# A 64 KiB input fetched by six transfers of 16, 8, 4, 2, 1 and 1 rows in place of one of 32 rows, beside an 8 MB load

## The chip, the cores and the metric

The kernel runs on one core of a Trainium2 chip. The metric is the device time of one execution in microseconds. The profile covers one execution; its span is about 2 us shorter than the time (782.8 against 784.6 us in the same execution). In the views DVE is VectorE, ACT is ScalarE, POOL is GpSimd and SP is SyncE; ACTq and SPq are what these two issue, and L57 is line 57 of that run's kernel.

## The reference

A mixture of four softmaxes: each of 32 x 128 positions has four rows of 4096 logits and four prior weights.

```python
logits: (32, 128, 4, 4096) float32      # 268 MB
prior:  (32, 128, 4)       float32      # 64 KiB
p   = softmax(prior,  axis=-1)          # over the 4 heads
s   = softmax(logits, axis=-1)          # over 4096
out = (p[..., None] * s).sum(axis=2)    # (32, 128, 4096) float32, 67 MB
```

## The kernel before

One batch is one 8 MB tile of 128 partitions x 4 heads x 4096. Each partition's part is one contiguous run of 64 KiB. Loads go through SyncE's DMA queue into two buffers, so the third load can start only when ScalarE has read the whole first tile. The prior goes through ScalarE's queue.

```python
    lpool = ctx.enter_context(tc.tile_pool(name="lpool", bufs=2))    # tiles of 8 MB
    epool = ctx.enter_context(tc.tile_pool(name="epool", bufs=2))    # results of the big Exps
    # ... cut
    load(0)                                             # SyncE's queue, 8 MB

    pr = cpool.tile([B, S, H], FP32, name="pr")
    nc.scalar.dma_start(out=pr, in_=prior)              # ScalarE's queue, 64 KiB
    load(1)                                             # SyncE's queue, 8 MB
    pmax = cpool.tile([B, S], FP32, name="pmax")
    nc.vector.reduce_max(pmax, pr, axis=AX.X)           # first reader of the prior
    pc = cpool.tile([B, S, H], FP32, name="pc")
    nc.vector.tensor_sub(pc, pr, pmax.unsqueeze(2).to_broadcast([B, S, H]))
    pe = cpool.tile([B, S, H], FP32, name="pe")
    nc.scalar.activation(pe, pc, AF.Exp)                # "the prior's Exp"
    # ... cut: sum, reciprocal and product pn, then 16 transposes of 32x32 into pp, all on VectorE

    for b in range(B):
        # ... cut: store(b - 1) from ScalarE's queue, the acc tile
        for h in range(H):
            # ... cut: et is a tile of epool, but for the last two batches
            nc.scalar.activation(et, lt[:, h], AF.Exp, accum_out=dsum)       # "big Exp"
            # ... cut
            nc.vector.reciprocal(rden, dsum)
            nc.vector.tensor_mul(coeff, rden, pp[:, h, b : b + 1])           # needs pp
            if h == 0:
                nc.vector.tensor_scalar_mul(out=acc, in0=et, scalar1=coeff)  # "the scaling"
            # ... cut: else acc = et * coeff + acc, "the accumulation"
        if b + 2 < B:
            load(b + 2)
        # ... cut: the last stores
```

The softmax here doesn't subtract the row's maximum and nothing guards it: scores larger than these inputs give would overflow.

## Time and profile before

| | before |
|---|---|
| time | 784.99 us, median of 3 runs (784.61 to 785.24) |
| DMA | 335.7 MB, 429 GB/s mean over the span |
| DVE busy / ACT busy | 70% / 60% |

These are lines of the page of before. The two rows of digits and numbers have 40 slices of the span. "DMA 73%" heads the chain of waits that ended last. The line of L60 is the reduce, the prior's first reader: after its busy time and mean stands its idle time and what ended it.

```profile
span 782.8 us, 977 instructions
...
DVE 544.9 (70%) x408; ACT 472.7 (60%) x258; POOL 0.2 (0%) x4
...
DMA  9999999999999999999999999999999999999997
GB/s 378 429 429 448 416 454 411 456 410 457 423 417 445 447 424 442 433 424 435 422 450 422 444 423 448 419 447 419 453 414 455 421 422 443 440 414 429 428 429 334
...
DMA 73%; DVE 18%; ACT 6%; issue 1%; DVEq 0%; ACTq 0%
...
L60 DVE TENSOR_REDUCE pmax<-pr 32x128 f32<-32x512 f32 x1 | 0.7, 673 | 11.5 <-DMA pr<-in_prior_dram 11.5
...
pr<-in_prior_dram ACTq DMA_DIRECT2D x1, 64.0 KB, 10.7
```

The DMA row is full in every slice but the last, while no compute engine is. A gap in this row cannot be made up later, because later slices have no room. The last line says that 64 KiB needed 10.7 us from issue to landing.

The next lines are of the timeline of before (start, duration, engine, what was done): the issues, the prior's reduce and transposes, then of the first batch the first big Exp, the scaling, the fourth big Exp and the store.

```profile
...
0.72 0.42 ACTq L57 DMA_DIRECT2D pr<-in_prior_dram  x1
0.73 39.20 SPq L45 DMA_DIRECT2D ltile<-in_logits_dram  x3
...
11.46 0.67 DVE L60 TENSOR_REDUCE pmax<-pr 32x128 f32<-32x512 f32 x1 [11.46 <-DMA pr<-in_prior_dram]
...
16.28 1.97 DVE L78 STREAM_TRANSPOSE pp<-pn 32x32 f32<-32x32 f32 x16
23.56 3.62 ACT L100 ACTIVATE etile<-ltile 128x4096 f32<-128x4096 f32 x1 [10.05 <-DMA ltile<-in_logits_dram]
...
27.70 2.35 DVE L106 TENSOR_SCALAR acc<-etile,coeff 128x4096 f32<-128x4096 f32 x1
...
35.87 3.62 ACT L100 ACTIVATE etile<-ltile 128x4096 f32<-128x4096 f32 x1 [1.40 <-DVE rden L103]
...
45.38 0.37 ACTq L51 DMA_DIRECT2D out_dram<-acc  x1
...
```

The first two loads keep the DMA engines full until about 42 us. The third load may go when the fourth big Exp has ended, at 39.5 us.

Below the views lie the trace's packet records (queue, start, duration, bytes; they do not name the engine). The prior's packets of before come in three rounds of 16, one per engine:

```
before, ScalarE's queue, by rounds
16 packets of 2048 B   start  4.75 to  5.50 us
16 packets of 2048 B   start  7.36 to  8.23 us
16 packets of    4 B   start 10.21 to 11.01 us    (the completions)
```

A completion is the 4-byte packet that follows an engine's rows; the prior's first reader starts 0.4 us after the last of them.

Between two rounds each engine moved one 64 KiB load packet (about 2.5 us; 2.42 us later, undisturbed). So a prior packet waits a "turn" of one load packet, whether it carries 2048 or 4 bytes.

### The profile page before, as it was taken

Reading aid. Unit: us, or ns where it says so; the run is one execution under the profiler, and the core shown is the slowest. Engines: PE = TensorE matmul, PEld = TensorE weight load, DVE = VectorE, ACT = ScalarE, POOL = GpSimd, SP = SyncE. Lnnn points to the kernel's source line nnn. Section 1 sums busy time; section 2 is a strip of 40 time slices with the busy share of each in tenths; the row PEclk is TensorE's granted clock in tenths of the full one; section 3 lists DMA queues with packets and bytes.
Section 4 is the critical chain, followed back from the end, with each engine's and each line's share of the span. In section 5 each row is a group of like instructions: output and inputs, shape, how many; then the busy total and the mean of one; then the engine's idle time right before and its main releaser. Section 6 shows DMA issues by size and latency. Waiting matters only on the chain.

```text
span 782.8 us, 977 instructions
## 1 busy us (share of the span) xinstructions
DVE 544.9 (70%) x408; ACT 472.7 (60%) x258; POOL 0.2 (0%) x4
## 2 busy tenths in 40 slices
DVE  3576687666786667866678666687666876669994
ACT  0766556755567555575555765556755567558971
POOL 0000000000000000000000000000000000000000
DMA  9999999999999999999999999999999999999997
GB/s 378 429 429 448 416 454 411 456 410 457 423 417 445 447 424 442 433 424 435 422 450 422 444 423 448 419 447 419 453 414 455 421 422 443 440 414 429 428 429 334
DMA packets 10712, 335.68 MB, mean 429 GB/s; under 512 B 1200, under 2 KB 1200, under 8 KB 1232
## 3 DMA queue, kind: packets, MB, share of 16 engines
q1 hardware_dynamic: 6624, 276.83, 82.0%
q10 hardware_dynamic: 4080, 58.79, 17.5%
q14 instruction: 8, 0.07, 0.0%
HBM read 268.50 MB, written 67.11 MB: 429 GB/s over the span
## 4 chain that ended last, share of the span: by engine, by line
DMA 73%; DVE 18%; ACT 6%; issue 1%; DVEq 0%; ACTq 0%
DMA ltile<-in_logits_dram 39%; DMA out_dram<-acc 34%; DVE acc L108 10%; ACT etile L100 6%; DVE ltile L108 3%; DVE acc L106 3%; DVE ltile L106 1%; DVE coeff L104 1%; DVE ltile L114 0%; DVE rden L103 0%; DVEq L152 0%; ACTq L100 0%; ACTq L51 0%; DVEq L106 0%
## 5 line engine op out<-in xcount | busy, mean ns | idle before, releaser
L100 ACT ACTIVATE etile<-ltile 128x4096 f32<-128x4096 f32 x120 | 433.4, 3612 | 276.3 <-DMA ltile<-in_logits_dram 203.9
L108 DVE SCALAR_TENSOR_TENSOR acc<-etile,coeff,acc 128x4096 f32<-128x4096 f32 x90 | 403.6, 4484 | 3.2
L103 DVE RECIPROCAL rden<-dsum 128x1 f32<-128x1 f32 x128 | 20.2, 158 | 156.3 <-ACT etile L100 156.3
L106 DVE TENSOR_SCALAR acc<-etile,coeff 128x4096 f32<-128x4096 f32 x30 | 70.6, 2353 | 50.1 <-DMA out_dram<-acc 50.0
L100 ACT ACTIVATE ltile<-ltile 128x4096 f32<-128x4096 f32 x8 | 28.9, 3610 | 4.8 <-DMA ltile<-in_logits_dram 2.2
L104 DVE TENSOR_TENSOR coeff<-rden,pp 128x1 f32<-128x1 f32 x128 | 20.4, 159 | 4.4
L108 DVE SCALAR_TENSOR_TENSOR ltile<-ltile,coeff 128x4096 f32<-128x4096 f32 x5 | 22.4, 4485 | 0.2
L100 ACT ACTIVATION_READ_ACCUMULATOR etile<-ltile 128x1 f32 x120 | 22.4, 186 | 0.0
L60 DVE TENSOR_REDUCE pmax<-pr 32x128 f32<-32x512 f32 x1 | 0.7, 673 | 11.5 <-DMA pr<-in_prior_dram 11.5
L64 ACT ACTIVATE pe<-pc 32x512 f32<-32x512 f32 x1 | 0.6, 628 | 10.4 <-DVE pc L62 10.4
L114 DVE SCALAR_TENSOR_TENSOR ltile<-ltile,coeff 128x1024 f32<-128x1024 f32 x4 | 4.9, 1281 | 0.0
L106 DVE TENSOR_SCALAR ltile<-ltile,coeff 128x4096 f32<-128x4096 f32 x2 | 4.7, 2353 | 0.1
L64 ACT ACT_TABLE_LOAD x1 | 1.3, 1283 | 1.2 <-PEq L141 1.2
L78 DVE STREAM_TRANSPOSE pp<-pn 32x32 f32<-32x32 f32 x16 | 1.9, 170 | 0.1
L100 ACT ACTIVATION_READ_ACCUMULATOR ltile<-ltile 128x1 f32 x8 | 1.5, 186 | 0.0
L66 DVE TENSOR_REDUCE psum<-pe 32x128 f32<-32x512 f32 x1 | 0.7, 674 | 0.7 <-ACT pe L64 0.7
L71 DVE TENSOR_TENSOR pn<-pe,prec 32x512 f32<-32x512 f32 x1 | 1.0, 1021 | 0.0
L68 DVE RECIPROCAL prec<-psum 32x128 f32<-32x128 f32 x1 | 0.9, 942 | 0.0
L62 DVE TENSOR_TENSOR pc<-pr,pmax 32x512 f32<-32x512 f32 x1 | 0.7, 678 | 0.0
L141 POOL MEMSET const-bfloat16-1.0<- 128x1 bf16 x1 | 0.1, 101 | 0.0
L141 POOL MEMSET const-uint8-127<- 128x1 uint8 x1 | 0.1, 101 | 0.0
L141 POOL MEMSET const-float32-0.0<- 128x1 f32 x1 | 0.1, 98 | 0.2 <-issue 0.2
(1 smaller groups left out, 0.1 us busy)
## 6 DMA issues: line engine op xcount, KB each, us to landing
out_dram<-acc ACTq DMA_DIRECT2D x28, 2048.0 KB, 30.0
ltile<-in_logits_dram SPq DMA_DIRECT2D x12, 2048.0 KB, 22.9
out_dram<-acc SPq DMA_DIRECT2D x2, 2048.0 KB, 34.1
out_dram<-ltile SPq DMA_DIRECT2D x1, 2048.0 KB, 22.8
out_dram<-ltile SPq DMA_DIRECT2D x2, 1024.0 KB, 10.2
ltile<-in_logits_dram SPq DMA_DIRECT2D x29, 31.3
pr<-in_prior_dram ACTq DMA_DIRECT2D x1, 64.0 KB, 10.7
```

The source lines that it names most:

```text
L60: nc.vector.reduce_max(pmax, pr, axis=AX.X)
L62: nc.vector.tensor_sub(pc, pr, pmax.unsqueeze(2).to_broadcast([B, S, H]))
L64: nc.scalar.activation(pe, pc, AF.Exp)
L68: nc.vector.reciprocal(prec, psum)
L71: nc.vector.tensor_mul(pn.rearrange("b h s -> b s h"), pe, prec.unsqueeze(2).to_broadcast([B, S, H]))
L78: nc.vector.transpose(pp[32 * t : 32 * (t + 1), h, :], pn[:, h, 32 * t : 32 * (t + 1)])
L100: nc.scalar.activation(et, lt[:, h], AF.Exp, accum_out=dsum)
L103: nc.vector.reciprocal(rden, dsum)
L104: nc.vector.tensor_mul(coeff, rden, pp[:, h, b : b + 1])
L106: nc.vector.tensor_scalar_mul(out=acc, in0=et, scalar1=coeff)
L108: nc.vector.scalar_tensor_tensor(out=acc, in0=et, scalar=coeff, in1=acc, op0=ALU.mult, op1=ALU.add)
L114: nc.vector.scalar_tensor_tensor(out=acc[:, cs], in0=et[:, cs], scalar=coeff, in1=acc[:, cs], op0=ALU.mult, op1=ALU.add,)
```

## The change

The intent: smaller first pieces, more transfers in flight, the same 64 KiB. Nothing else changes, and the order of all other instructions on all engines stays.

```diff
     pr = cpool.tile([B, S, H], FP32, name="pr")
-    nc.scalar.dma_start(out=pr, in_=prior)
+    for lo, hi in ((16, 32), (8, 16), (4, 8), (2, 4), (1, 2), (0, 1)):
+        nc.scalar.dma_start(out=pr[lo:hi], in_=prior[lo:hi])
     load(1)
```

## The prediction

> **What bounds the kernel now.** Data transfer. The page's DMA row is at nine tenths or more in all slices but the last, 429 GB/s mean for 335.7 MB; DVE is busy 70%, ACT 60%. The chain of waits is 73% DMA. In the trace's packet records a load packet is one 64 KiB row; an undisturbed one takes 2.42 us, so 16 engines give 433 GB/s, and 335.7 MB need 775 of the 782.8 us. A stretch with empty engines is paid in full. Before the third load, by the timeline, the first two loads keep the engines full until about 42 us, and ACT releases the third at about 39.5 us: a margin of 2.5 us.
>
> **What the change does.** No bytes go away. One DMA issue on ACT's queue (0.42 us) becomes six (about 2.5 us, while ACT has nothing to do: free). The order of the other instructions is unchanged; DMA semaphores are handed out five places later, but each is again met long after its earlier transfer landed: zero.
>
> The cost is the prior's landing, which competes with the first 8 MB load. In the packet records of before each engine carries two 2 KiB prior rows and one 4-byte completion, each behind one 64 KiB load packet, starting at about 4.9, 7.6 and 10.3 us; the reduce waits 11.46 us. This agrees with the Trainium skill, "DMA: Bandwidth & Descriptors", Queues, rings and completion order: engines alternate between queues packet by packet. The same page (Why a DMA increments its semaphore by 16) says that a transfer uses the largest engine count up to 16 that divides its slowest dimension, on the lowest-numbered engines. Then all six pieces put a row and a completion on the first engine: 12 packets instead of 3, each behind a load packet. No run has shown this yet.
>
> Estimate: from 4.9 us, 11 more turns at 2.4 to 2.85 us (one fewer where the load's own completion takes the turn): last completion at about 31.3 us, reduce at 31.7 us instead of 11.46.
>
> **On the critical path.** The prior's Exp stands before the first big Exp on ACT. Its chain (0.67+0.68+0.63 us) ends at about 33.8 us, so the first big Exp starts there, not at 23.56. The transposed prior is ready at about 38.5 us (18.25 before). Repeating the first batch's timeline (Exp 3.6, scale 2.35, accumulate 4.48, two Exp buffers), the fourth Exp ends at about 49.9 us instead of 39.5. The third load's packets start at about 51 us instead of 41.8: engines nearly empty for some 8.5 us from 42.5 us. The rest repeats shifted by about 9 us; nothing gives it back, as the engines are full to the end.
>
> **Prediction: 794.2 us**, 80% range 785.5 to 799.0. Faster by over 2%: 0.01. Within 2%: 0.92. Slower by over 2%: 0.07.
>
> **What would show it.** Right: the prior's reduce waits about 31.5 us; small prior packets spaced by a load packet until about 31 us; first big Exp at about 34 us; DMA share near zero from 43 to 51 us; busy times and the later 24 us per batch unchanged. Wrong step: the prior lands near 11 to 16 us (pieces not stacked, or several small packets per turn), and the time stays at 785. Wrong size: prior late, but the gap shorter, or later slices denser.
>
> **What would make it wrong.** Pieces might start on different engines; a turn may carry several small packets; a late start might find slack that I do not see. One-row pieces may be cut across all engines, which leaves the first engine's count.

## More of the kernel before

All runs quoted here are with a granted clock of 1.000.

The window view of before has, per window, the busy time of DVE, ACT and POOL, the clock, then the DMA share and GB/s:

```profile
...
core 0: us, DVE busy (x) ACT busy (x) POOL busy (x), PEclk, DMA share, GB/s
40.00:42.00 2.00, 1.93 (x4) 0.00 (x0) 0.00 (x0) 1.00 0.84 360
42.00:44.00 2.00, 2.00 (x1) 0.00 (x0) 0.00 (x0) 1.00 0.46 197
44.00:46.00 2.00, 1.35 (x1) 0.14 (x1) 0.00 (x0) 1.00 1.21 524
46.00:48.00 2.00, 0.00 (x0) 2.00 (x1) 0.00 (x0) 1.00 1.25 524
48.00:50.00 2.00, 0.33 (x3) 2.00 (x3) 0.00 (x0) 1.00 1.27 541
...
```

A packet is counted by its start, and a load packet of 64 KiB takes longer than a window. So single windows swing around 1. What matters is that none is near zero: the third load follows the second without a pause.

## The result, and the profile after

| | before | after |
|---|---|---|
| time, median of 4 | 784.89 us (784.61 to 785.24) | 793.52 us (793.24 to 795.87) |
| prior's reduce starts | 11.46 us | 30.59 us |
| transposed prior ready | 18.25 us | 37.40 us |
| first packet of the third load | 41.71 us | 49.75 us |

The ratio is 1.0116, 95% interval 1.0096 to 1.0136. A ratio here is the mean time of one kernel's runs over that of the other's of the same rounds, so it is not quite the ratio of the medians (1.0110). The change costs 8.6 us, 1.1%, which is within 2%.

The same lines of the page after. (The chain of waits is not shown: in this profile it can be followed back only through the last 6% of the span.)

```profile
span 791.9 us, 987 instructions
...
DVE 546.3 (69%) x408; ACT 470.9 (59%) x258; POOL 0.2 (0%) x4
...
DMA  9959999999999999999999999999999999999997
GB/s 377 467 218 424 409 444 456 405 459 414 445 420 444 436 434 420 428 460 408 454 411 449 435 425 456 418 434 417 456 410 454 414 444 449 415 421 434 427 430 331
...
L61 DVE TENSOR_REDUCE pmax<-pr 32x128 f32<-32x512 f32 x1 | 0.7, 675 | 30.6 <-DMA pr<-in_prior_dram 30.6
...
```

The reduce now waits 30.6 us, and the third slice of the DMA row falls to five tenths, 218 GB/s. All other slices of that row are as before; busy times of DVE and ACT differ by less than 2 us. From 60 to 720 us both kernels move 433 GB/s by the window view. So nearly all of the loss is one gap at the start.

The timeline after:

```profile
...
0.72 2.25 ACTq L58 DMA_DIRECT2D pr<-in_prior_dram  x6
0.73 48.39 SPq L45 DMA_DIRECT2D ltile<-in_logits_dram  x3
...
30.59 0.68 DVE L61 TENSOR_REDUCE pmax<-pr 32x128 f32<-32x512 f32 x1 [30.59 <-DMA pr<-in_prior_dram]
...
32.55 3.60 ACT L101 ACTIVATE etile<-ltile 128x4096 f32<-128x4096 f32 x1
...
35.44 1.96 DVE L79 STREAM_TRANSPOSE pp<-pn 32x32 f32<-32x32 f32 x16
...
37.83 2.35 DVE L107 TENSOR_SCALAR acc<-etile,coeff 128x4096 f32<-128x4096 f32 x1
...
45.06 3.62 ACT L101 ACTIVATE etile<-ltile 128x4096 f32<-128x4096 f32 x1 [1.07 <-DVE rden L104]
...
54.57 0.38 ACTq L51 DMA_DIRECT2D out_dram<-acc  x1
...
```

All of the first batch's compute is later, and the third load waits for it. The windows after:

```profile
...
core 0: us, DVE busy (x) ACT busy (x) POOL busy (x), PEclk, DMA share, GB/s
40.00:42.00 2.00, 1.93 (x4) 1.72 (x1) 0.00 (x0) 1.00 0.00 0
42.00:44.00 2.00, 2.00 (x1) 1.99 (x2) 0.00 (x0) 1.00 0.00 0
44.00:46.00 2.00, 1.93 (x4) 0.94 (x1) 0.00 (x0) 1.00 0.00 0
46.00:48.00 2.00, 2.00 (x1) 2.00 (x1) 0.00 (x0) 1.00 0.00 0
48.00:50.00 2.00, 1.97 (x3) 0.77 (x2) 0.00 (x0) 1.00 0.98 328
...
```

Four windows stand at zero, the first of them only because its packets had started before 40 us. By the packet records the second load's last packet ends at 42.05 us and the third load's first starts at 49.75 us: 7.7 us with empty engines, at a stage where before had none. Here is why the prior is late, from the records:

```
after, ScalarE's queue, by rounds
16 x 2048 B at  4.8-5.1     16 x 4 B at  7.5-7.9     (16 rows)
 8 x 2048 B at  9.9-10.3     8 x 4 B at 12.5-12.9    (8 rows)
 4 x 2048 B at 15.0-15.3     4 x 4 B at 17.6-17.8    (4 rows)
 2 x 2048 B at 20.0-20.1     2 x 4 B at 22.5-22.6    (2 rows)
 1 x 2048 B at 22.52         1 x 4 B at 25.02        (1 row)
 1 x 2048 B at 27.45         1 x 4 B at 29.94        (1 row)
```

Each transfer puts one row on each of as many engines as it has rows. The spacing stays that of a load packet, 2.4 to 2.7 us, all the way to the last completion: on the engine with most packets, 12 prior packets in ten such steps of 2.5 us on average and one step without a wait. This is what one finds if one engine takes part in all six transfers and alternates: one prior packet, one load packet. That one step, at 22.5 us, also fits: there the first load's own completion (4 bytes) took the load's turn.

### The profile page after: what moved, and what is told of

Read it like the earlier page. It is cut to its first block, busy times and chain, and to the rows that moved or that the text cites. A ratio compares the mean times of both kernels' runs of the same rounds, so it can differ in the third digit from the quotient of the medians.

```text
span 791.9 us, 987 instructions
## 1 busy us (share of the span) xinstructions
DVE 546.3 (69%) x408; ACT 470.9 (59%) x258; POOL 0.2 (0%) x4
## 3 DMA queue, kind: packets, MB, share of 16 engines
q10 hardware_dynamic: 4096, 58.79, 17.3%
## 5 line engine op out<-in xcount | busy, mean ns | idle before, releaser
L61 DVE TENSOR_REDUCE pmax<-pr 32x128 f32<-32x512 f32 x1 | 0.7, 675 | 30.6 <-DMA pr<-in_prior_dram 30.6
```

## The experiments

Theory ("turns"): a prior packet waits one load packet of its engine; the engine with the most prior packets decides when the prior has landed; from there a fixed chain of compute leads to the third load; past a break-even this opens a gap in the DMA, paid in full. Rivals: (A) each extra transfer costs by itself; (B) the six transfers shift the semaphores which later transfers use by five places, and this costs (a semaphore is what the program makes an engine wait on until a transfer has landed); (C) the gap comes from ScalarE's order, where the prior's Exp stands before the big ones; (D), which no run was made for: the six transfers do not share an engine but follow one another, each starting when the one before has wholly landed.

All outputs are right. All runs are in three rounds with the kernel before on the same chip. Four kernels of one submission (two34, fine6, fine1, spfirst6) were run by no chip the first time and were sent again, unchanged, as the runs ending in "b".

### Two transfers of 16 rows (two16)

```diff
-    for lo, hi in ((16, 32), (8, 16), (4, 8), (2, 4), (1, 2), (0, 1)):
+    for lo, hi in ((16, 32), (0, 16)):
```

> Two transfers of 16 rows. Turn theory (each packet of the prior waits one 64 KiB load packet on its engine; the engine with the most packets decides): 4 packets on every engine (row, completion, row, completion), starting at about 4.9, 7.5, 10.0 and 12.6 us, so the prior's reduce starts at about 13.2 us; break-even is a start at 22.5 us, so the time stays that of before, 785 us. Rival (each extra transfer costs by itself, 8.6 us over 5 extra ones = 1.7 us each): 786.6 us. Rival (the shifted semaphore places cost): some loss, of unknown size.

Measured: 785.15 us against 784.71; ratio 1.0011 (0.9994 to 1.0028): no cost. The reduce starts at 14.07 us, 0.9 us later than expected, as some turns took 2.9 us. One more turn is free, because the prior has slack.

### Four transfers, 8 packets on the busiest engine (four8)

```diff
-    for lo, hi in ((16, 32), (8, 16), (4, 8), (2, 4), (1, 2), (0, 1)):
+    for lo, hi in ((16, 32), (8, 16), (4, 8), (0, 4)):
```

> Four transfers of 16, 8, 4 and 4 rows. Turn theory: 8 packets on the first four engines, the last starting at about 22.5 us, the reduce at about 23.1 us, just past the break-even of 22.5 us: 785 to 786 us. Rival (cost per transfer): three extra transfers, 790.1 us, the same as the next run of four transfers.

Measured: 786.75 us against 784.71; ratio 1.0026 (1.0011 to 1.0041). The reduce starts at 23.68 us, the third load's packets at 42.85 us. This is 0.75 us above the range that was expected, and far below the 790.1 of rival A.

### Five transfers, 10 packets (five10)

```diff
-    for lo, hi in ((16, 32), (8, 16), (4, 8), (2, 4), (1, 2), (0, 1)):
+    for lo, hi in ((16, 32), (8, 16), (4, 8), (2, 4), (0, 2)):
```

> Five transfers of 16, 8, 4, 2 and 2 rows: 10 packets on the first two engines. Turn theory: last packet at about 25.0 us, reduce at about 25.6 us, 3.1 us past break-even, so the third load starts at about 44.8 us and the time is about 788.3 us (787.5 to 789). Rival (cost per transfer): 791.8 us.

Measured: 788.82 us against 784.71; ratio 1.0057 (1.0042 to 1.0072). The timeline of this run has the reduce where it was expected:

```profile
...
25.50 0.67 DVE L61 TENSOR_REDUCE pmax<-pr 32x128 f32<-32x512 f32 x1 [25.50 <-DMA pr<-in_prior_dram]
...
```

The third load's packets start at 44.66 us, as expected (44.8). Rival A's 791.8 us is off by 3 us. Dropping the last split of two rows into 1 and 1 thus saves 4.5 us of the 8.6, each against before in its own rounds.

The records of this run also speak against rival D. The fourth transfer's two completions start at 22.16 and 22.40 us, the fifth's two rows at 22.18 and 22.41 us. So the fifth transfer's first row starts before the fourth has wholly landed, and each row comes right behind one completion, as on a shared engine.

### Four transfers, 12 packets in count (four12): a miss

```diff
-    for lo, hi in ((16, 32), (8, 16), (4, 8), (2, 4), (1, 2), (0, 1)):
+    for lo, hi in ((7, 32), (3, 7), (1, 3), (0, 1)):
```

> Four transfers of 25, 4, 2 and 1 rows. 25 rows can be split over 5 engines only, so the first engine has 5+1, 1+1, 1+1 and 1+1 = 12 packets, as many as the changed kernel has with six transfers. Turn theory: last packet at about 30 to 30.5 us, reduce at 30.6 to 31.2 us, 793.5 to 794.5 us, as the changed kernel. Rival (cost per transfer): 790.1 us, the same as the run of 16, 8, 4 and 4 rows.

Measured: 785.05 us against 784.71; ratio 1.0008 (0.9993 to 1.0023). The theory's number failed by 9 us, and rival A's by 5. The packet records of the profiled run (its time was 786.72 us, the other three 784.65 to 785.33) show that 25 rows did go to five engines, five rows each, as expected, but not all of them waited:

```
four12, ScalarE's queue
20 x 2048 B at 1.69-3.28     5 x 2048 B at 5.5-5.8     then turns, last completion at 22.97
```

Twenty rows went at once, and then five together one load packet later. So four rows on each of five engines were on their way before those engines had started their first 64 KiB load packet. Four turns were saved, the reduce started at 23.64 us, and this run cost 2.0 us, as four8 with its 8 packets did. The three other runs cost nothing that shows; they left no trace, so what was different in them is not known. The count of packets was right, but "each behind a load packet" was not: packets that are there first wait for nothing.

### The same four transfers, held back (four12late), and their control (four8late)

Both kernels write the prior's tile once on VectorE and ScalarE first. Its transfers must wait for that, and are issued at 2.7 us and not at 0.7.

```diff
     pr = cpool.tile([B, S, H], FP32, name="pr")
+    nc.vector.memset(pr, 0.0)
+    nc.scalar.activation(pr, pr, AF.Exp)
-    for lo, hi in ((16, 32), (8, 16), (4, 8), (2, 4), (1, 2), (0, 1)):
+    for lo, hi in ((7, 32), (3, 7), (1, 3), (0, 1)):         # four12late
+    for lo, hi in ((16, 32), (8, 16), (4, 8), (0, 4)):       # four8late
```

> The run of 25, 4, 2 and 1 rows missed: in its records four of the five rows of the 25-row piece reached their engines before those had their first load packet, and passed without waiting, so only 8 of 12 packets took turns. Here the same four transfers are held until ScalarE has written the prior's tile once (a fill and an Exp, some 2 us), so that the load comes first. Turn theory: all 12 packets wait, the first starts at about 4.8 us or one turn later, the reduce at 30.5 to 33.5 us, the third load's packets 19.2 us after it, and 793.5 to 796.5 us. Rival (a count of packets or of engines does not matter, 25 rows are simply cheaper): 785 us.

> Control of the run before it: the same delay by ScalarE, and also four transfers, but of 16, 8, 4 and 4 rows, so 8 packets on the busiest engines. Turn theory: reduce at 23.5 to 26 us, 786.5 to 789 us, some 7 us less than the run before it. If the delay itself or the number of transfers made the time: the same time as that run.

Measured: four12late 797.34 us against 784.76, ratio 1.0177 (1.0132 to 1.0222; one of its runs took 802.85 us), which leaves open whether it is over 2%. four8late 786.99 us, ratio 1.0038 (1.0001 to 1.0076; one of its runs took 791.25 us). The reduce in the timelines of four12late and then of four8late:

```profile
...
33.28 0.68 DVE L63 TENSOR_REDUCE pmax<-pr 32x128 f32<-32x512 f32 x1 [31.90 <-DMA pr<-in_prior_dram]
...
23.85 0.67 DVE L63 TENSOR_REDUCE pmax<-pr 32x128 f32<-32x512 f32 x1 [22.48 <-DMA pr<-in_prior_dram]
...
```

Now all five rows of the 25-row piece wait: their rounds start at 7.2, 9.7, 12.2, 14.8 and 17.5 us, and the last completion at 32.63 us. The third load's packets start at 52.45 us. The reduce came within the range expected; the time is 0.8 us above it. With the same number of transfers and the same delay, 8 packets cost 2.2 us and 12 packets 12.6 us, a larger step than the 7 us expected. Number and delay of the transfers are excluded as the cause; how many turns are taken is what counts.

### 31 rows and 1 row (two34b)

```diff
-    for lo, hi in ((16, 32), (8, 16), (4, 8), (2, 4), (1, 2), (0, 1)):
+    for lo, hi in ((1, 32), (0, 1)):
```

> (Second try of the run of 31 and 1 rows, which no chip ran; since then the transfer of 25 rows has been measured to cost nothing, so the divisor reading is in doubt.) Two transfers of 31 and 1 rows. If the engine count is the largest divisor up to 16 of 31, which is 1, the first engine holds 34 packets: reduce at 43 to 46 us and 805 to 811 us. If odd row counts are split otherwise (near evenly over the engines, as few packets on each), the reduce starts at 13 to 16 us and the time is 785 us. Rival (cost per transfer): 786.6 us.

The doubt named there came from the times of four12 alone; its records settle it, as the 25 rows end in five completions. Measured: 808.14 us against 785.02; ratio 1.029 (1.0266 to 1.0314). Only two transfers, and the largest loss of all. The timeline:

```profile
...
44.52 0.67 DVE L61 TENSOR_REDUCE pmax<-pr 32x128 f32<-32x512 f32 x1 [44.52 <-DMA pr<-in_prior_dram]
...
```

The records show one prior packet at a time: 7 rows by 2.6 us, before the engine's first load packet, then one per turn from 5.38 us, and the last 9 rows within 0.7 us from 43.28 us, once the loads had nothing more to send. So all 31 rows sat on one engine, and turns, not bytes, took the time. The third load's packets start at 63.68 us.

### Six transfers beside small load packets (fine6b, control fine1b)

```diff
-    load(0)
+    lt = lpool.tile([P, H, V], FP32, name="ltile")
+    for c in range(0, V, V // 2):
+        nc.sync.dma_start(out=lt[:, :, c : c + V // 2], in_=logits[0, :, :, c : c + V // 2])
+    ltiles[0] = lt
     # fine6b: the six prior transfers as in the change; fine1b: one of 32 rows
```

> The six transfers of the changed kernel, but the first batch's load comes as two transfers of half the columns of each head, so its packets are 8 KiB and not 64 KiB (turn of about 0.3 us). Turn theory: the 12 packets of the first engine pass within some 4 to 6 us, the reduce starts at about 8 to 11 us and the time is that of before, 785 us. If the six transfers cost by their number, by their small size or by the semaphore places: still about 793.5 us.

> Control of the run before it: the same two column halves for the first load, and the prior in one transfer. Turn theory: reduce at 6 to 8 us, and 785 us, within 0.5 us of the run with six transfers. If the finer first load gains or loses time by itself, it shows here against the kernel before.

Measured: fine6b 785.87 us, ratio to before 1.0006 (0.9983 to 1.0028); fine1b 784.95 us, ratio 0.9992 (0.9970 to 1.0013). The timeline of fine6b:

```profile
...
9.11 0.67 DVE L64 TENSOR_REDUCE pmax<-pr 32x128 f32<-32x512 f32 x1 [9.11 <-DMA pr<-in_prior_dram]
...
```

With 8 KiB load packets the same six transfers have landed at 9.1 us and not at 30.6, and the loss is gone. In fine1b, the reduce starts at 2.55 us and not at the 6 to 8 us expected, because all its prior packets (1.76 to 2.14 us) start before the load's first (2.18 us); the time is that of before: an earlier prior gains nothing. In fine6b too the first transfer's rows and most of its completions start before the load's first packet (2.16 us), so the edit changed a second thing besides the packet size; but ten packets of the busiest engine still had to pass beside the load. They did not pass at one load packet each throughout: between the second transfer's last completion (4.32 us) and the third's first row (5.70 us) 69 load packets started, about four on each engine. Why is not known. The 0.9 us between fine6b and fine1b is above the 0.5 us that was expected; the intervals of both hold 1, and its cause is open. Rival A falls here, as it did in two34b: this kernel has all six transfers and even one more load transfer, without the loss.

### Six transfers ahead of the first load in its own queue (spfirst6b)

```diff
-    load(0)
     pr = cpool.tile([B, S, H], FP32, name="pr")
     for lo, hi in ((16, 32), (8, 16), (4, 8), (2, 4), (1, 2), (0, 1)):
-        nc.scalar.dma_start(out=pr[lo:hi], in_=prior[lo:hi])
+        nc.sync.dma_start(out=pr[lo:hi], in_=prior[lo:hi])
+    load(0)
```

> The six transfers issued from SyncE's queue ahead of the first load, so they stand before it in the same queue and nothing is to be waited for. Turn theory: reduce at about 5 to 6 us. The first load is issued 2.25 us later than before (six issues), so its packets and everything behind them start about 2.3 us later: 787 us (786.5 to 788). Rivals (number of transfers, semaphore places): 793.5 us or more.

Measured: 786.37 us against 785.02; ratio 1.0009 (0.9983 to 1.0035), a little under the range expected. The reduce is earlier than expected too:

```profile
...
3.98 0.68 DVE L60 TENSOR_REDUCE pmax<-pr 32x128 f32<-32x512 f32 x1 [3.98 <-DMA pr<-in_prior_dram]
...
```

The first load's packets start 2.0 us later than before (3.74 against 1.74 us); the median is 1.35 us above before's. Standing first in the queue cures nearly all of it. The semaphores of later transfers are shifted here too, and by the trace the transfers from the second load on use the same ones as in the changed kernel, so rival B falls with this run.

### Two big Exps ahead of the prior's Exp (expfirst6)

```diff
+    early = {}                                    # ahead of the prior's chain
+    for h in range(2):
+        # ... cut: tiles et and dsum, as in the loop
+        nc.scalar.activation(et, ltiles[0][:, h], AF.Exp, accum_out=dsum)
+        early[h] = et, dsum
+    # ... cut: tile zero
+    nc.vector.tensor_scalar_mul(out=zero, in0=early[1][1][:B], scalar1=0.0)
     pmax = cpool.tile([B, S], FP32, name="pmax")
     # ... cut
-    nc.scalar.activation(pe, pc, AF.Exp)
+    nc.scalar.activation(pe, pc, AF.Exp, bias=zero)
     # ... cut: for b == 0 and h < 2 the loop takes et and dsum from early
```

> The changed kernel with the first two big Exps ahead of the prior's Exp in ScalarE's order (a zero bias made from the second sum holds that order). It asks which part of the late prior delays the third load. If ScalarE's order is what binds, the first batch gains up to about 8 us and the time goes back towards 785 us. If VectorE's chain from the reduce to the transposed prior binds (the first scaling needs it, and the third big Exp needs the buffer that the scaling frees), the first Exp starts at 23.6 us, but the first scaling at about 38 us as in the changed kernel, the third load's packets at about 49.8 us, and the time stays at 793.5 to 794.5 us.

Measured: 794.85 us against 784.78; ratio 1.0127 (1.0111 to 1.0144), 0.35 us above the range expected if VectorE's chain binds. The timeline, with the two early Exps, the reduce, the first scaling and the fourth big Exp:

```profile
...
23.15 3.62 ACT L64 ACTIVATE etile<-ltile 128x4096 f32<-128x4096 f32 x1 [18.84 <-DMA ltile<-in_logits_dram]
...
26.76 3.60 ACT L64 ACTIVATE etile<-ltile 128x4096 f32<-128x4096 f32 x1
...
30.49 0.67 DVE L69 TENSOR_REDUCE pmax<-pr 32x128 f32<-32x512 f32 x1 [30.49 <-DMA pr<-in_prior_dram]
...
37.71 2.35 DVE L118 TENSOR_SCALAR acc<-etile,coeff 128x4096 f32<-128x4096 f32 x1
...
44.67 3.62 ACT L112 ACTIVATE etile<-ltile 128x4096 f32<-128x4096 f32 x1 [0.81 <-DVE rden L115]
...
```

The first big Exp starts 9.4 us earlier than in the changed kernel (23.15 against 32.55 us), yet the scaling starts at 37.71 against 37.83 us, and the third load's packets at 49.38 against 49.75 us. Rival C falls: ScalarE's idle time was the visible symptom, but the scaling waits for the transposed prior, and the third Exp for the buffer that the scaling frees.

### All runs on one line

| run | packets that took turns on the busiest engine | reduce starts | third load's first packet | difference | median, less before's |
|---|---|---|---|---|---|
| four8 | 8 | 23.68 us | 42.85 us | 19.17 | +2.0 us |
| four12, its profiled run | 8 | 23.64 us | 42.81 us | 19.17 | +2.0 us (the run; the median +0.3) |
| four8late | 8, first one turn later, last without a wait | 23.85 us | 43.02 us | 19.17 | +2.2 us |
| five10 | 10 | 25.50 us | 44.66 us | 19.16 | +4.1 us |
| changed kernel | 12 | 30.59 us | 49.75 us | 19.16 | +8.6 us |
| four12late | 12, first one turn later | 33.28 us | 52.45 us | 19.17 | +12.6 us |
| two34b | 17, then the loads had ended | 44.52 us | 63.68 us | 19.16 | +23.1 us |
| before / two16 | 3 / 4 | 11.46 / 14.07 us | 41.71 / 42.03 us | (the second load's end decides) | 0 / +0.4 us |

From the reduce to the third load it is 19.16 to 19.17 us in every kernel of the table past the break-even (18.89 us in expfirst6, whose edit changes this chain). The break-even is at 41.71 - 19.16 = 22.55 us. Past it the time grows with the reduce's start, microsecond for microsecond, plus 0.6 to 1.8 us (in the medians: the last column less the shift of the third load from 41.71 us). Part of that extra is that the first packets after an empty stretch take longer (2.57 to 3.27 us in the changed kernel, against 2.42); the rest was not isolated.

## Why the prediction was right, point by point

- **The landing.** Predicted: 12 packets on the first engine, each behind a load packet, last completion at 31.3 us, reduce at 31.7. Measured: last completion 29.94 us, reduce 30.59. The mechanism held, with the load's own completion taking one turn, as the prediction had allowed. The size was off by 1.1 to 1.4 us, since a turn took about 2.5 us nearly throughout, not up to 2.85. That the shared engine is "the first" is not shown, as the records name none; that one engine takes part in all six is inferred from the rounds, above all from those of five10 and two34b.
- **The path.** Predicted: first big Exp at 33.8, transposed prior at 38.5, fourth Exp ended at 49.9, third load's packets at 51 us. Measured: 32.55, 37.40, 48.68 and 49.75 us. All are the landing's 1.1 to 1.3 us early. The prediction listed both ScalarE's late start and the late transposed prior; expfirst6 shows that only the second binds.
- **The gap.** Predicted about 8.5 us from 42.5 us. Measured 7.7 us from 42.05.
- **Nothing given back.** Held: 433 GB/s from 60 to 720 us in both. 794.2 us was predicted, 793.52 measured. The good match owes something to two errors that cancel: the landing 1.1 us too late, and the slow first packets after the gap left out.
- **Free parts.** Six issues took 2.25 us of ScalarE's queue (2.5 predicted), while it had nothing to do. The shifted semaphores cost nothing that shows in spfirst6b.
- **Where the theory failed on the way.** "Each behind one load packet" holds only once the load has started on that engine. In four12 four rows per engine, in two34b seven, got ahead. For the changed kernel it made no difference: its first row starts at 4.76 us, behind a load packet. The prediction took that over from before and did not ask whether it would hold, so this part was fortunate.

No run beats before by a clear margin: the prior had 11 us of slack (22.55 less 11.46), and the DMA engines were full anyway.

## What to carry to other kernels

A small transfer that runs beside a large one does not cost its bytes, but, with the 64 KiB load packets, one packet of the large one for each of its own packets on its busiest engine, completions included (fine6b, with 8 KiB packets, was less regular). Count these packets, multiply by the large packet's duration, and compare with the time at which the data are needed. Keep small inputs in one transfer whose row count spreads over all engines, issue them ahead of the bulk load in the same queue (tried with six transfers only, whose issues held the load back by 2.0 us), or cut the bulk load's first packets smaller. And when an engine idles before a late input, find what the next stage truly waits for before moving that engine's work.

## What the Trainium skill lacked or had wrong

- "DMA: Bandwidth & Descriptors", Queues, rings and completion order, gives a typical packet as 9 to 17 descriptors, and its section SWDGE vs HWDGE vs iDMA, of the packets that GpSimd builds, prefers at most 4096 bytes. Here, with transfers issued from SyncE and ScalarE, a load packet was one row of 65,536 bytes, and each prior row and each completion took a turn of its own (rounds 2.4 to 2.9 us apart). The alternation packet by packet, as the page has it, agrees with all runs but fine6b, where one round waited for about four load packets.
- The page has no warning of what follows from that: a 64 KiB transfer beside a load with 64 KiB packets landed at 11 us as one transfer and at 30 us as six. Its Rules for kernel authors do say to merge many small transfers, which is right here too, but for the reason that under 64 KB one pays mostly overhead; in fine1b the same 64 KiB, in one transfer ahead of the load's packets, was there at 2.55 us, so here it was waiting and not overhead.
- The rule for the engine count in Why a DMA increments its semaphore by 16 agrees for 32, 16, 8, 4 and 2 rows, for 25 rows (five engines) and for 31 rows (one engine). For a single row of 512 elements its words ("slowest non-size-1 dim") could be read as 16 engines; the records show one packet of 2048 bytes.
- No page says that a transfer on few engines can get ahead of a load issued at the same time: 20 rows in four12 and 7 in two34b started before their engines' first load packet, while beside 64 KiB packets the 16- and 32-row pieces did not (first start at 4.7 us or later). The cause is open.
